# Token-major projections of a split-fp32 encoder layer: both weight parts in one 512-column matmul, halves added on VectorE, epsilon on GpSimd

## The chip, the cores and the metric

The kernel runs on one core of one Trainium2 chip. The metric is the time on the device in microseconds (us). Three runs of the kernel before took 1884.93, 1879.48 and 1882.31 us, so its median is 1882.31 us. The profile is of one more execution, whose span from the first to the last instruction is 1880.0 us.

Names of the engines: PE is TensorE's matmuls, PEld its weight loads, DVE is VectorE, ACT is ScalarE, POOL is GpSimd, SP is SyncE, which issues the DMAs.

## The reference

One encoder layer is applied to two groups (prompt and sample) of 1024 tokens and 1024 channels, with the same weights. Cut to what matters:

```
h = rms_norm(x, norm_g) * (1 + scale) + shift          # scale, shift, gate from w_ada
proj = einsum('bsd,de->bse', h, w_in)                  # one projection, split into
qa, ka, va, za, qb, kb, vb, zb, ga, gb = split(proj)   # 512,128,128,512, 512,512,512,512, 1024,1024
qa, ka = rope_2d(rms_norm(qa)), rope_2d(rms_norm(ka))  # per head of 64 channels, eps 1e-6
oa = gqa_attention(qa, ka, va) * silu(za)              # 8 query heads, 2 key heads
qb, kb = rope(rms_norm(qb)), rope(rms_norm(kb))        # 4 heads, two maps each
ob = rms_norm(diff_attention(qb, kb, vb, lam)) * silu(zb)
merged = sigmoid(ga) * (oa @ w_proj_a) + sigmoid(gb) * (ob @ w_proj_b)
y = x + gate * (merged @ w_out)
```

All data is float32. The kernel multiplies with a reduced float32 type and keeps the accuracy by splitting each operand into a high part and a low part (value minus high part): a product is high x high + high x low + low x high, three matmuls.

## The kernel before, in words

**The weave.** The two groups run one after the other. In each, a head computes K and V of branch A and half of branch A's queries, then the attention units run, woven with work that does not depend on them ("filler": the rest of the projections and the gate paths), then come the merge and the output projection. `weave` takes pieces of several generators in turn, by counts given in tables at the top; a generator's `yield` ends a piece. Afterwards a scheduler with its own model of the engines orders the instructions of each engine, and lets the attention's instructions go ahead by a priority. The order on each engine is fixed then; each engine works through its own in that order.

**Two kinds of projections.** The gate paths (`z_gen`, matmul at L764) hold a piece of the weights still and move 512 tokens; their result has channels on the partitions. The token-major projections (`proj_tt`, matmul at L574) hold 128 tokens still and move 256 weight columns; their result has tokens on the partitions, 128 tokens x 256 channels. A weight tile `w` has, for each of 8 chunks of 128 input channels, 256 columns of the high part and then 256 columns of the low part. For each chunk `proj_tt` issues three matmuls of 256 columns (L574): token high part x weight high part, token high part x weight low part, token low part x weight high part. All 24 of a tile add up in the same 256 columns of one PSUM bank. Each has its own weight load, also where two in a row hold the same tokens.

**How many.** Each group has 8 token tiles of K and V of branch A (`kva_gen`), 2 x 8 of branch A's queries (`qa_gen`), 4 x 8 of branch B's queries and keys (`qkb_gen`), 2 x 8 of branch B's values (`vb_gen`): 72, so 144 in the kernel, 3456 matmuls at L574. 112 of them (all but the values of B) go through `rms`.

**What follows a tile.** `rms`: ACT copies the bank into a row tile in SBUF (L591), ACT squares it (L592), DVE sums each head's squares (L595), DVE adds epsilon (L596), POOL raises to the power -0.5 (L597). `rope` (L620 to L626) and the products with the gains run on DVE in the head (`alone`) and on POOL later. Two tiles later `pairs_T` transposes the row on PE (L637) into a PSUM bank, from which ACT (L639) and DVE (L640) write the high and low parts of the queries and keys. `vb_gen` only copies (L749); in `kva_gen` V is a second copy out of the bank (L689).

**Banks.** Projections, transposes and some small products take turns in three PSUM banks (`ps_f`, tiles f); the scores have two double banks (`ps_s`, tiles s); the values of the attention one (`ps_a`). While `alone` holds, two in five of the gate-path and transposing tiles take an s bank. A bank that is still read cannot be written.

**The attention.** A score step is four 512-column matmuls (L798, L799), a maximum on DVE (L800, 1024 columns), a product (L801), the exponential on ACT (L802), and a transposition on DVE (L843) that goes through DMAs (L852) to the values' matmuls (L866, L883). There are 256 score steps.

Of the kernel before, what the change touches and what calls it, by code (L numbers as in the profile page):

```python
# [14 lines left out]
AF = mybir.ActivationFunctionType  # L15
ALU = mybir.AluOpType
# [9 lines left out]
HD = 64  # L26
EPS = 1e-6
# [62 lines left out]
def kernel(ctx: ExitStack, tc: tile.TileContext, t: dict):  # L90
    nc = tc.nc
# [17 lines left out]
    def nm(s):  # L109
        uid[0] += 1  # L110
        return f"{s}_{uid[0]}"
# [13 lines left out]
    def fbank():  # L125
        return ps_f.tile([P, 512], F32, tag="f", name=nm("f"))

    def utile():
        return upool.tile([P, 2048], F32R, tag="u", name=nm("u"))
# [24 lines left out]
    def rtile():  # L154
        return mtile("row", [P, 512], bufs=3)
# [18 lines left out]
    def behind(ins, other):  # L174
        dep = mybir.DependencyInfo(mybir.DependencyClass.NoSync, mybir.DependencyReason.DATA)
        tc.add_manual_dep(ins.ins, other.ins.name, dep)
# [30 lines left out]
    def load_w(pieces, early=False):  # L207

        w = wpool.tile([P, NCH, 2, 256], F32R, tag="w", name=nm("w"))
        sts = []  # L210
        for q in range(4):
            if early:
                if q % 2 == 0:
                    room = halves2(ptile())
                st = room[q % 2].rearrange("p (c n) -> p c n", c=2)
            else:
                st = spool.tile([P, 2, 256], F32, tag="st", name=nm("st"))
            sts.append(st)
            off = 0
            for src in pieces(q):  # L220
                n = src.shape[1]
                dma(st[:, :, off : off + n], src.rearrange("(c p) n -> p c n", p=P))
                off += n
            assert off == 256
            if not early:
                split_w(w, q, st)
        return (w, sts) if early else w

    def w_cols(mat, *cols):
        def pieces(q):  # L230
            return [mat[q * 256 : (q + 1) * 256, c : c + n] for c, n in cols]
        return pieces
# [330 lines left out]
    latest = [None]  # L563

    def proj_tt(ht, w, tt):
        ps = fbank()[:, :256]
        hh, hl = ht[tt // 4]
        sl = slice((tt % 4) * P, (tt % 4 + 1) * P)
        k = 0
        for c in range(NCH):  # L570
            if c in CUTS:
                yield 1
            for lt, wi in ((hh, 0), (hh, 1), (hl, 0)):
                ins = nc.tensor.matmul(ps, lt[c][:, sl], w[:, c, wi, :], start=(k == 0), stop=(k == 23))  # L574
                if latest[0] is None:
                    behind(ins, picked[0])
                latest[0] = ins
                k += 1
        return ps

    def by_turns(tt):

        return nc.vector if alone[0] else nc.gpsimd

    chained = [None, None]

    def rms(ps, nh, e, kept=None, first=0):
        n = nh * HD
        row = rtile()
        raw, sq = row[:, :n], row[:, 256 : 256 + n]  # L590
        nc.scalar.activation(raw, ps, AF.Copy)  # L591
        chained[0] = nc.scalar.activation(sq, raw, AF.Square, scale=1.0 / math.sqrt(HD))  # L592
        ss = tiny.tile([P, 4], F32, tag="ss", name=nm("ss"))[:, :nh]
        rs = kept if kept is not None else tiny.tile([P, 4], F32, tag="rs", name=nm("rs"))[:, :nh]
        nc.vector.tensor_reduce(out=ss, in_=sq.rearrange("p (h d) -> p h d", d=HD), axis=AX.X, op=ALU.add)  # L595
        nc.vector.tensor_scalar(out=ss, in0=ss, scalar1=EPS, scalar2=None, op0=ALU.add)  # L596
        nc.gpsimd.tensor_tensor(out=rs, in0=ss, in1=nhalf[:, :nh], op=ALU.pow)  # L597
        raw3 = raw.rearrange("p (h d) -> p h d", d=HD)
        if first < nh:
            e.tensor_tensor(  # L600
                out=raw3[:, first:], in0=raw3[:, first:],
                in1=rs[:, first:].unsqueeze(2).to_broadcast([P, nh - first, HD]), op=ALU.mult,
            )
        return raw3, sq.rearrange("p (h d) -> p h d", d=HD)

    def rope(x3, s3, cos, sin, half, e):

        nh = x3.shape[1]
        w = x3.shape[2]
        ng = w // (2 * half)  # L610
        c3 = mtile("rc", [P, 4, HD], bufs=1)[:, :nh, :w]
        if len(cos.shape) == 3:
            x4, s4, c4 = (t.rearrange("p (a m) d -> p a m d", a=2) for t in (x3, s3, c3))
            cs, sn = (t.unsqueeze(2).to_broadcast([P, 2, nh // 2, w]) for t in (cos, sin))
        else:
            x4, s4 = (t.rearrange("p h (g d) -> p h g d", g=ng) for t in (x3, s3))
            c4, cs = None, None
            sn = sin.rearrange("p (g d) -> p g d", g=ng).unsqueeze(1).to_broadcast([P, nh, ng, 2 * half])
        if c4 is None:
            e.tensor_tensor(out=c3, in0=x3, in1=cos.unsqueeze(1).to_broadcast([P, nh, w]), op=ALU.mult)  # L620
        else:
            e.tensor_tensor(out=c4, in0=x4, in1=cs, op=ALU.mult)
        for a in range(2):
            o, i = (slice(b * half, (b + 1) * half) for b in (a, 1 - a))
            e.tensor_tensor(out=s4[..., o], in0=x4[..., i], in1=sn[..., o], op=ALU.mult)
        chained[1] = e.tensor_tensor(out=x3, in0=c3, in1=s3, op=ALU.add)  # L626
# [3 lines left out]
    def pairs_T(x3, even, odd):  # L630


        nb = x3.shape[1] // 2
        ps = gbank()[:, : nb * P].rearrange("p (b n) -> p b n", b=nb)
        x = x3.rearrange("p (b two) d -> p b (two d)", two=2)
        for b in range(nb):
            nc.tensor.transpose(ps[:, b, :], x[:, b, :], ident)  # L637
        for dst, hi, lo in ((even, LO, HI), (odd, HI, LO)):
            nc.scalar.activation(dst[hi], ps[hi], AF.Copy)  # L639
            nc.vector.tensor_tensor(out=dst[lo], in0=ps[hi], in1=dst[hi].bitcast(F32), op=ALU.subtract)  # L640
# [3 lines left out]
    def pipelined(ht, w, front, back, fill=(TAIL_Z, TAIL_Z)):  # L644
        pend = []
        for tt in range(NTT):
            ps = yield from proj_tt(ht, w, tt)
            pend.append((tt, front(tt, ps)))
            if tt == NTT - 1 and not alone[0]:
                ends[:] = chained  # L650
            if len(pend) > LAG:
                back(*pend.pop(0))
            yield 1
        while pend:
            for _ in range(fill[alone[0]]):
                next(filler[0], None)
            yield 1
            back(*pend.pop(0))
        yield 1
# [14 lines left out]
    def v2(u):  # L674
        return u.rearrange("p (h n) -> p h n", h=2)

    def kva_gen(ht, out):
        w = kva_w.pop()[0] if kva_w else load_w(w_cols(w_in, (C_KA, 256)))
        k = v2(utile())
        u = utile().bitcast(F32)  # L680
        va = u[:, :1024].rearrange("p (n k d) -> p n k d", n=NTT, k=2)
        out["ka"], out["va"] = k, va
        out["rsA"] = u[:, 1024 : 1024 + 2 * NTT * 4].rearrange("p (a n h) -> p a n h", a=2, n=NTT)

        def front(tt, ps):
            e = by_turns(tt)
            x3, s3 = rms(ps[:, :128], 2, e)
            vp = ps[:, 128:256].rearrange("p (k d) -> p k d", k=2)
            nc.scalar.activation(va[:, tt], vp, AF.Copy)  # L689
            e.tensor_tensor(out=x3, in0=x3, in1=gka.unsqueeze(1).to_broadcast([P, 2, HD]), op=ALU.mult)  # L690
            rope(x3, s3, out["cosA"][:, tt], out["sinA"][:, tt], 16, e)
            return x3

        def back(tt, x3):
            sl = slice(tt * P, (tt + 1) * P)
            pairs_T(x3, k[:, 0:1, sl], k[:, 1:2, sl])

        yield from pipelined(ht, w, front, back, (0, 0))
# [44 lines left out]
    def vb_gen(ht, out, pr):  # L743
        w = load_w(w_cols(w_in, (C_VB + pr * 256, 256)))
        v = utile().bitcast(F32).rearrange("p (n h e) -> p n h e", n=NTT, h=2)
        out[2 * pr], out[2 * pr + 1] = v[:, :, 0], v[:, :, 1]
        for tt in range(NTT):
            ps = yield from proj_tt(ht, w, tt)
            nc.scalar.activation(v[:, tt].rearrange("p h e -> p (h e)"), ps, AF.Copy)  # L749
            yield 1  # L750


# [527 lines left out]
    for g in range(2):  # L1280
# [19 lines left out]

        phase(0, qa_gen(st, 1))
        phase(1, vb_gen(ht, st["vb"], 0), qkb_gen(st, 0))
        oT, mT = ([], []), ([], [])
        for h in range(4):
# [8 lines left out]
        first = chain(*[gated_gen(st, i, hf, oT[hf]) for i in range(2) for hf in range(2)])  # L1313
# [78 lines left out]
```

## Time and profile before

| | |
|---|---|
| three runs | 1879.48, 1882.31, 1884.93 us |
| the profiled execution, span | 1880.0 us |
| PE busy, DVE busy | 1836.5 us, 1222.3 us |
| ACT busy, POOL busy | 780.1 us, 607.1 us |
| matmuls in the trace, of them at L574 and at L764 | 10398, 3456, 2304 |
| granted TensorE clock, mean | 0.995 of full |

The profile lists groups of instructions with the names of the tiles they write and read, their number, their total busy time and the mean of one. The record of a matmul is longer than the step from one matmul to the next, because matmuls are pipelined: the step is read from rows that give a run of matmuls with its length. The profiled execution is told by its span; nothing before the first or after the last instruction is in it.

### The profile page before, as it was taken

The numbers are of one execution on the slowest core, as the hardware profiler recorded it, in microseconds if no ns is written. First come the engines' busy times: TensorE is split into PE (matmuls) and PEld (weight loads), VectorE is DVE, ScalarE is ACT, GpSimd is POOL, SyncE is SP. The second block draws the span as 40 slices with busy tenths as digits, with TensorE's granted clock in tenths as the row PEclk, the third lists the DMA queues.
The fourth block names the chain that finished last, engine by engine and source line by source line (L and its number), as shares of the span: only waits on it lengthen the run. The fifth ranks groups of instructions, "written<-read, shape, count | busy, mean of one in ns | idle before, by whom it ended". The sixth has DMA issues, their size and how long they took to land.

```text
span 1880.0 us, 29891 instructions
## 1 busy us (share of the span) xinstructions
PE 1836.5 (98%) x10398; PEld 1550.6 (82%) x10398; DVE 1222.3 (65%) x2016; ACT 780.1 (41%) x1544; POOL 607.1 (32%) x888
## 2 busy tenths in 40 slices
PE   6999999999999999999999999999999999999999
PEld 3798877888899977888889888888888898888887
DVE  5777766454777777347466687666357766663795
ACT  4544434344554444313223445344345545442241
POOL 1243311433454451221233333014354635222100
PEclk8999999999999999999999999999999999999999
DMA  9135776555444567754631567666524343675442
GB/s 324 57 94 160 208 198 178 146 168 163 111 127 113 162 188 219 244 152 140 206 131 52 156 177 204 189 186 188 158 68 141 106 129 103 176 247 173 128 127 92
DMA packets 283895, 295.46 MB, mean 157 GB/s; under 512 B 41952, under 2 KB 236640, under 8 KB 283744
## 3 DMA queue, kind: packets, MB, share of 16 engines
q1 hardware_dynamic: 283744, 293.54, 53.1%
q8 instruction: 83, 1.36, 0.3%
q14 instruction: 68, 0.56, 0.1%
HBM read 133.98 MB, written 42.01 MB: 94 GB/s over the span
## 4 chain that ended last, share of the span: by engine, by line
PE 68%; DMA 4%; issue 3%; DVE 3%; SPq 3%; POOL 2%; ACT 1%; ACTq 0%; DVEq 0%; POOLq 0%
PE f L764 15%; PE f L574 15%; PE f L1038 7%; PE a L883 5%; PE s L798 4%; PE s L799 4%; PE a L866 4%; PE s L1038 3%; PE f L1073 3%; PE s L1073 2%; PE f L1145 2%; SPq L852 1%; DMA q<-p 1%; DMA st<-in_w_in_dram 1%; PE s L1145 1%
## 5 line engine op out<-in xcount | busy, mean ns | idle before, releaser
L764 PE MATMUL f<-u,w 128*128 128x512 f32 x2232 | 565.1, 395 | 0.8 <-POOL w L197 0.4
L574 PE MATMUL f<-w,u 128*128 128x256 f32 x3456 | 478.6, 287 | 0.9 <-POOL w L197 0.4
L764 PEld LDWEIGHTS f<-u,w 128*128 128x128 f32 x2232 | 409.8, 188 | 82.6 <-POOL w L197 1.1
L574 PEld LDWEIGHTS f<-w,u 128*128 128x128 f32 x3456 | 452.3, 193 | 22.3 <-issue 3.5
L800 DVE TENSOR_REDUCE m<-s 128x1 f32<-128x1024 f32 x256 | 309.6, 1218 | 98.8 <-PE s L799 97.4
L197 POOL TENSOR_TENSOR w<-st,w 128x512 fp32r<-128x512 f32 x160 | 213.2, 1350 | 357.9 <-ACT w L195 342.1
L843 DVE STREAM_TRANSPOSE p<-p 128x1024 f32<-128x1024 f32 x192 | 237.7, 1243 | 87.9 <-ACT p L802 73.5
L802 ACT ACTIVATE p<-s,m,u 128x1024 f32<-128x1024 f32 x128 | 153.9, 1204 | 160.0 <-issue 57.8
L802 ACT ACTIVATE p<-s,m,rsB 128x1024 f32<-128x1024 f32 x128 | 154.0, 1204 | 118.7 <-DVE m L801 97.1
L799 PE MATMUL s<-u,sw 128*128 128x512 f32 x512 | 201.1, 397 | 0.0
L195 ACT ACTIVATE w<-st 128x512 fp32r<-128x512 f32 x184 | 108.2, 626 | 112.4 <-DMA st<-in_w_in_dram 97.5
L1038 PE MATMUL f<-u,w 128*128 128x512 f32 x552 | 131.0, 392 | 0.0
L883 PE MATMUL a<-q,u 128*128 128x256 f32 x512 | 126.5, 380 | 4.0 <-DMA q<-p 3.7
L597 POOL TENSOR_TENSOR rsB<-ss,nhalf 128x4 f32<-128x4 f32 x64 | 68.1, 1064 | 184.7 <-DVE ss L596 160.6
L866 PE MATMUL a<-q,u 128*64 128x256 f32 x1024 | 117.7, 382 | 3.6 <-DMA q<-p 2.9
L1038 PEld LDWEIGHTS f<-u,w 128*128 128x128 f32 x552 | 103.0, 188 | 21.1
L798 PE MATMUL s<-u 128*128 128x512 f32 x256 | 107.9, 425 | 2.7 <-ACT p L802 2.7
L799 PEld LDWEIGHTS s<-u,sw 128*128 128x128 f32 x512 | 96.5, 189 | 16.4
L640 DVE TENSOR_TENSOR u<-f,u 64x256 fp32r<-64x256 f32 (+1 forms) x198 | 81.3, 411 | 42.9 <-ACT u L639 37.5
L883 PEld LDWEIGHTS a<-q,u 128*128 128x128 f32 x512 | 93.5, 190 | 18.8 <-issue 3.4
L772 ACT ACTIVATE ev<-f 128x512 f32<-128x512 f32 x93 | 55.3, 595 | 128.5 <-PE f L764 72.5
L866 PEld LDWEIGHTS a<-q,u 128*64 128x64 f32 x1024 | 73.8, 137 | 40.3 <-issue 7.2
(221 smaller groups left out, 2174.6 us busy)
## 6 DMA issues: line engine op xcount, KB each, us to landing
q<-p SPq DMA_DIRECT2D x768, 128.0 KB, 2.6
st<-in_w_in_dram SPq DMA_DIRECT2D x132, 256.0 KB, 3.3
zd<-ev SPq DMA_DIRECT2D x96, 256.0 KB, 2.7
sw<-u SPq DMA_DIRECT2D x256, 64.0 KB, 2.0
u<-in_w_ada_dram SPq DMA_DIRECT2D x8, 1024.0 KB, 11.7
oo<-zd SPq DMA_DIRECT2D x64, 128.0 KB, 2.4
od<-oo SPq DMA_DIRECT2D x64, 128.0 KB, 2.4
st<-in_w_in_dram SPq DMA_DIRECT2D x64, 128.0 KB, 2.7
```

The lines of the kernel that those rows point to most:

```text
L195: hi = nc.scalar.activation(wh, st, AF.Copy)
L197: lo = e.tensor_tensor(out=wl, in0=st, in1=wh.bitcast(F32), op=ALU.subtract)
L574: ins = nc.tensor.matmul(ps, lt[c][:, sl], w[:, c, wi, :], start=(k == 0), stop=(k == 23))
L764: ins = nc.tensor.matmul(ps, w[:, c, wi, e * P : (e + 1) * P], rt[c], start=(k == 0), stop=(k == 23),)
L798: nc.tensor.matmul(s[:, sl], q, k[:, sl], start=True, stop=False)
L799: nc.tensor.matmul(s[:, sl], sw, k[:, sl], start=False, stop=True)
L800: nc.vector.tensor_reduce(out=m, in_=s, axis=AX.X, op=ALU.max, negate=True)
L802: nc.scalar.activation(pt.rearrange("p (j c a) -> p j c a", j=4, c=8), s.rearrange("p (c a j) -> p j c a", c=8, j=4), AF.Exp, bias=m, scal ...
L843: nc.vector.transpose(pt, pt)
L866: lambda k=k, m=m: nc.tensor.matmul(acc[(LO, HI)[m]], u["v"][:, k], pT[m][:, k], start=(k == 0), stop=(k == 7))
L883: nc.tensor.matmul(acc, u["v"][:, k], pT[:, k], start=(k == 0), stop=(k == 7))
L1038: nc.tensor.matmul(ps, w[:, c, wi, d * P : (d + 1) * P], o[:, oi, :], start=(k == 0), stop=(k == 11))
```

## The change

The token-major projections use a whole PSUM bank. The token high part meets both weight parts in one matmul of 512 columns (the two parts lie next to each other in `w`), which fills both halves of the bank; the token low part meets the weight high part in a matmul of 256 columns that adds into the second half. A chunk has two matmuls and two weight loads where it had three of each, a tile 16 where it had 24. The number of columns that go through PE is the same.

What follows must add the halves: ACT copies the first half to SBUF, and DVE adds the second half, out of PSUM, to it (`summed`). In `kva_gen` V is copied from the summed row, not from PSUM. The addition of epsilon moves from DVE to POOL.

```
     def proj_tt(ht, w, tt):
-        ps = fbank()[:, :256]
+        ps = fbank()
...
-            for lt, wi in ((hh, 0), (hh, 1), (hl, 0)):
-                ins = nc.tensor.matmul(ps, lt[c][:, sl], w[:, c, wi, :], start=(k == 0), stop=(k == 23))
+            both = w[:, c].rearrange("p s n -> p (s n)")
+            for lt, out, wt in ((hh, ps, both), (hl, ps[:, 256:], w[:, c, 0, :])):
+                ins = nc.tensor.matmul(out, lt[c][:, sl], wt, start=(k == 0), stop=(k == 15))
...
+    def summed(out, ps):
+
+        nc.scalar.activation(out, ps[:, :256], AF.Copy)
+        nc.vector.tensor_tensor(out=out, in0=out, in1=ps[:, 256:], op=ALU.add)
...
-    def rms(ps, nh, e, kept=None, first=0):
+    def rms(ps, nh, e, kept=None, first=0, vp=None):
...
-        nc.scalar.activation(raw, ps, AF.Copy)
+        summed(row[:, :256], ps)
+        if vp is not None:
+            nc.scalar.activation(vp, row[:, n:256].rearrange("p (h d) -> p h d", d=HD), AF.Copy)
...
-        nc.vector.tensor_scalar(out=ss, in0=ss, scalar1=EPS, scalar2=None, op0=ALU.add)
+        nc.gpsimd.tensor_scalar(out=ss, in0=ss, scalar1=EPS, scalar2=1.0, op0=ALU.add, op1=ALU.mult)
...
-            x3, s3 = rms(ps[:, :128], 2, e)
-            vp = ps[:, 128:256].rearrange("p (k d) -> p k d", k=2)
-            nc.scalar.activation(va[:, tt], vp, AF.Copy)
+            x3, s3 = rms(ps, 2, e, vp=va[:, tt])
...
-            nc.scalar.activation(v[:, tt].rearrange("p h e -> p (h e)"), ps, AF.Copy)
+            summed(v[:, tt].rearrange("p h e -> p (h e)"), ps)
```

In the changed kernel the lines from 574 on have other numbers: the matmul of `proj_tt` is L575, the copy L584, the addition of the halves L585, the sum of squares L603, epsilon L604, the power L605, the transposition L645, the score matmuls L804 and L805, the maximum L806.

The scheduler orders each engine anew. PE at one place of the first group, in the weave of branch B: f_6714 is a projection tile, f_6791 the next one, f_6768 a bank of transposes, s_6942 a score step. Before:

```order
L574 MATMUL f_6714<-w_6462,u_329 128x256
L637 MATMUL f_6768<-ident,row_6604 128x128 x2
L798 MATMUL s_6942<-u_5427 128x512
L799 MATMUL s_6942<-u_5427,sw_6709 128x512
L798 MATMUL s_6942<-u_5427 128x512
L799 MATMUL s_6942<-u_5427,sw_6709 128x512
L574 MATMUL f_6791<-w_6462,u_511 128x256 x2
```

The same two projection tiles of the changed kernel are f_6245 and f_6315; f_6292 is the bank of transposes, s_6452 and s_6480 are two score steps:

```order
L575 MATMUL f_6245<-w_6014,u_329 128x256
L804 MATMUL s_6452<-u_5091 128x512
L805 MATMUL s_6452<-u_5091,sw_6240 128x512
L804 MATMUL s_6452<-u_5091 128x512
L805 MATMUL s_6452<-u_5091,sw_6240 128x512
L804 MATMUL s_6480<-u_5092 128x512
L805 MATMUL s_6480<-u_5092,sw_6240 128x512
L804 MATMUL s_6480<-u_5092 128x512
L805 MATMUL s_6480<-u_5092,sw_6240 128x512
L645 MATMUL f_6292<-ident,row_6141 128x128 x2
L575 MATMUL f_6315<-w_6014,u_497 128x512
```

Between one projection tile and the next there stand eight score matmuls instead of four; the transposes have moved behind them.

DVE at the same place. Before, row_6754 is the SBUF row of the projection tile f_6714, m_6941 the maximum of the score step s_6942:

```order
L801 TENSOR_TENSOR m_6873<-m_6873,rsB 128x1
L640 TENSOR_TENSOR u_6484<-f_6687,u_6484 64x2x128
L800 TENSOR_REDUCE m_6941<-s_6942 128x1
L827 RECIPROCAL r_6882<-su_6872 128x1
L640 TENSOR_TENSOR u_6483<-f_6768,u_6483 64x2x128
L595 TENSOR_REDUCE ss_6757<-row_6754 128x4
L801 TENSOR_TENSOR m_6941<-m_6941,rsB 128x1
L596 TENSOR_SCALAR ss_6757<-ss_6757 128x4
```

In the changed kernel row_6277 is the row of f_6245, m_6451 the maximum of s_6452:

```order
L807 TENSOR_TENSOR m_6387<-m_6387,rsB 128x1
L585 TENSOR_TENSOR row_6277<-row_6277,f_6245 128x256
L806 TENSOR_REDUCE m_6451<-s_6452 128x1
L833 RECIPROCAL r_6396<-su_6386 128x1
L603 TENSOR_REDUCE ss_6281<-row_6277 128x4
L806 TENSOR_REDUCE m_6479<-s_6480 128x1
L807 TENSOR_TENSOR m_6451<-m_6451,rsB 128x1
```

The addition of the halves stands ahead of the maximum of the score step that PE does after the tile; the epsilon row is gone from DVE.

## The prediction

> **What bounds the kernel now.** I read the page's busy times first, then PE's waits, then the stretches, then the chain of work that ended last. The page gives the span and the share of each engine:
>
> ```profile
> span 1880.0 us, 29891 instructions
> PE 1836.5 (98%) x10398; PEld 1550.6 (82%) x10398; DVE 1222.3 (65%) x2016; ACT 780.1 (41%) x1544; POOL 607.1 (32%) x888
> ```
>
> PE has work at 98% of the time, the other engines at two thirds or less. Since matmul records overlap, that alone does not show that PE sets the end. The view of waits of PE does: these are the longest but for the ones of the start, and together they are 18.3 us of 1880.
>
> ```profile
> PE s L798 <- ACT p L802: 4.2, 6, 1.2
> PE a L883 <- DMA q<-p: 3.7, 4, 1.5
> PE f L637 <- POOL row L626: 3.4, 2, 3.2
> PE a L866 <- DMA q<-p: 2.9, 4, 1.3
> PE f L637 <- DVE row L626: 2.5, 2, 1.4
> PE s L637 <- DVE row L626: 1.6, 1, 1.6
> ```
>
> The other engines wait for PE instead. ACT's copy of a projection tile, in the view of all waits, stood ready 71 times and waited for the tile's last matmul:
>
> ```profile
> ACT row L591 <- PE f L574: 138.1, 71, 6.8
> ```
>
> By stretches (PE, PEld, DVE, ACT, POOL busy us, then granted clock, DMA share, GB/s) the head of the first group is the place where PE has most pauses and DVE least; the weave of branch B in the second group is typical of the rest:
>
> ```profile
> 46.00:120.00 74.00, 69.42 (x470) 63.05 (x470) 60.52 (x173) 36.74 (x102) 26.38 (x28) 0.98 0.17 51
> 1280.00:1600.00 320.00, 315.13 (x1921) 275.41 (x1921) 200.94 (x341) 152.84 (x309) 150.70 (x281) 1.00 0.45 125
> ```
>
> DVE is at 82% in the first and at 63% in the second, where PE is at 98% and the clock is full. So the kernel is a queue of matmuls, and what a matmul takes from PE counts nearly in full, as long as the work behind it keeps up.
>
> **What the matmuls lose.** How long a step from matmul to matmul is, I take from the chain of waits, which gives unbroken runs (start us, length us, count):
>
> ```profile
> 801.98 24.48 PE f L1038 x108
> ...
> 893.80 10.88 PE f L1073 x48
> ...
> 970.89 8.64 PE f L574 x72
> ...
> 1019.02 5.75 PE f L574 x48
> ```
>
> A 512-column matmul steps by 24.48 / 108 = 226.7 ns, and L1073 by the same 10.88 / 48; the 256-column one of the projections by 8.64 / 72 = 120.0 ns, and 5.75 / 48 = 119.8. Half of 226.7 is 113.3, so the narrow matmul costs 6.7 ns more than its half. Put otherwise, 256 columns more cost 106.7 ns, and 13.3 ns come with each matmul, wide or narrow. A chunk is now 3 x 120.0 = 360.0 ns. The changed chunk is one wide and one narrow, 226.7 + 120.0 = 346.7 ns: 13.3 ns less, the fixed part of the matmul that goes. With 144 tiles of 8 chunks, 1152 chunks, that is **15.3 us off PE**. That a narrow one next to a wide one keeps its 120 ns is seen where a projection tile is followed by a gate-path tile:
>
> ```profile
> 370.04 3.04 PE L574 MATMUL f<-w,u 128*128 128x256 f32 x24
> 372.91 0.40 PE L764 MATMUL f<-u,w 128*128 128x512 f32 x1
> ```
>
> 24 narrow steps, the last one to a wide matmul, take 2.87 us, 119.6 each. The two rows give ends for the saving: nothing, if the wide matmul took two narrow steps, and 360.0 - 1.5 x 226.7 = 20.0 ns a chunk, 23.0 us, if the narrow one took half a wide one. I take the sum of the two measured steps.
>
> The Trainium skill speaks against this size: "TensorE: Matmul & The Clock Gate", section "Back-to-back issue gap", gives a warm step of N / 2.4 + 2.5 ns. By it a chunk would go from 327.5 to 325.0 ns, and the change would save 2.9 us in all. The trace's steps of 226.7 and 120.0 ns do not agree with it: the part that does not grow with the columns is 13.3 ns here.
>
> The 1152 weight loads that go lie under matmuls and are worth nothing by themselves; nothing takes their place.
>
> **What is added.** The rows that are nearest to the new DVE addition (128x256, one operand in PSUM, one in SBUF), the removed epsilon, and the new POOL epsilon are these:
>
> ```profile
> L872 DVE TENSOR_TENSOR oo<-a,oo 128x256 f32<-128x256 f32 x32 | 13.3, 416 | 39.6 <-PE a L866 39.5
> L596 DVE TENSOR_SCALAR ss<-ss 128x4 f32<-128x4 f32 x96 | 21.3, 222 | 1.3
> L900 POOL TENSOR_SCALAR suB<-suB 128x8 f32<-128x8 f32 x8 | 2.5, 309 | 0.7
> L626 DVE TENSOR_TENSOR row<-rc,row x32: 280/424/1268, 56.0 to 1043.9; 128x128 f32<-128x128 f32 x16, 128x256 f32<-128x256 f32 x16
> ```
>
> L872 has the new addition's size and kinds of operands: 0.416 us. The far end is 1.27 us, the longest L626, of the same size with both operands in SBUF; I take 0.416, which is the same form. (The Trainium skill, "SBUF — State Buffer", section "Who interferes with whom", says that a DVE instruction with two SBUF inputs can be blocked by GpSimd and that one with a single SBUF input cannot; L626's 1268 beside its median of 424 agrees with the first half.) DVE gets 144 x 0.416 = 59.9 us more and loses at most 112 x 0.222 = 24.9, so 1222 becomes about 1257 us, 67% of the span. POOL gets 112 x 0.31 = 35 us, 34%. ACT keeps its count but for a wider first copy in the 16 tiles of K and V, at 41%. None of these totals reaches PE's; what can cost is the length of the chain behind a tile, at three places.
>
> *The bank.* A projection bank is now held until DVE has added: 0.42 us longer if DVE is free, and if DVE is in a transposition, up to this row's mean more:
>
> ```profile
> L843 DVE STREAM_TRANSPOSE p<-p 128x1024 f32<-128x1024 f32 x192 | 237.7, 1243 | 87.9 <-ACT p L802 73.5
> ```
>
> So 0.42 to 1.66 us. Where room was short before, PE's weight load was held by the copy alone, as here (the bank of f_6714, then f_6791):
>
> ```profile
> 648.29 0.38 ACT L591 ACTIVATE row<-f 128x256 f32<-128x256 f32 x1
> ...
> 648.73 0.42 PEld L574 LDWEIGHTS f<-w,u 128*128 128x128 f32 x3 [0.30 <-ACT row L591]
> ```
>
> The new order of PE puts eight score matmuls where four stood between these two tiles, four times 226.7 ns or 0.9 us more room, so the scheduler pays for most of the longer hold. The same addition stands ahead of the next score maximum on DVE: queued behind it are that maximum, ACT's exponential and the next use of the score bank. PE needs 0.9 us for the score step anyway, and the addition 0.42. I put 2 us on banks, and 0 to 8 as ends (nothing to 0.42 us at 19 tiles, one in eight).
>
> *The transposes.* Five waits of L637 for the row are in the waits of PE above, 7.5 us together. Their rows come later by the addition and by the epsilon, 0.42 + 0.31 - 0.22 = 0.5 us each: 2.5 us, with 0 to 5 as ends (they vanish by the new order, or there are ten).
>
> *The head.* DVE is nearly full where query tiles follow each other with nothing between. One period of PE, and DVE's work in it:
>
> ```profile
> 106.69 3.12 PE L574 MATMUL f<-w,u 128*128 128x256 f32 x24
> ...
> 107.17 0.42 DVE L620 TENSOR_TENSOR rc<-row,tab 128x256 f32<-128x256 f32 x1 [0.22 <-ACT row L591]
> ...
> 107.63 0.42 DVE L640 TENSOR_TENSOR u<-f,u 64x256 fp32r<-64x256 f32 x1
> 108.08 0.42 DVE L595 TENSOR_REDUCE ss<-row 128x4 f32<-128x256 f32 x1
> ...
> 108.53 0.17 DVE L596 TENSOR_SCALAR ss<-ss 128x4 f32<-128x4 f32 x1
> 108.61 0.51 DVE L625 TENSOR_TENSOR row<-row,tab 128x128 f32<-128x128 f32 x2
> 109.15 0.43 DVE L640 TENSOR_TENSOR u<-f,u 64x256 fp32r<-64x256 f32 x1
> 109.61 0.43 DVE L626 TENSOR_TENSOR row<-rc,row 128x256 f32<-128x256 f32 x1
> 109.78 3.11 PE L574 MATMUL f<-w,u 128*128 128x256 f32 x24
> ```
>
> The period is 109.78 - 106.69 = 3.09 us and DVE works 2.80 of it. With the change PE's period is 3.09 - 8 x 0.0133 = 2.98 and DVE's work 2.80 + 0.42 - 0.17 = 3.05: DVE is the slower by 0.07 us a tile. Only a few tiles follow each other like this, so DVE falls back by a few tenths of a microsecond and does not stop PE, whose transposes come two tiles later. In the stretch before, where PE pauses most, the addition lies on the way of the K tiles' rows. I put 1 us on the head of both groups, 0 to 4 as ends.
>
> **The sum.** -15.3 + 2 + 2.5 + 1 = -9.8 us, so the profiled execution's 1880.0 us would become 1870.2. The span lies 2.3 us under the median of the runs, so the prediction is **1872 us**. With the ends of the added costs alone it is 1867 to 1884.
>
> **The rivals.**
>
> *The chain takes more than PE saves (slower).* ACT copies, DVE adds, and only then is the bank free; DVE is in order and has 1.2 us instructions in it. If each of the 71 tiles whose copy waited for PE gave its 0.416 us on to PE, that is 29.5 us, and the time 1882.3 - 15.3 + 29.5 = 1896. It decides from 15.3 / 144 = 0.11 us of PE wait per tile. For it speaks that the head's DVE has no room; against it the small waits of PE for banks and rows now, and the new order.
>
> *The wide matmul takes two narrow steps.* Then 240 ns stand in place of 226.7, PE saves nothing, the added 5.5 us stay: 1888. Against it are the two runs at 226.7 ns, of the same kind of operands. The skill's rule above is the near end of this: 2.9 us saved, 1885.
>
> *The narrow matmul shrinks as well.* 113.3 ns beside a wide one: 23.0 us less, and with half of the added costs 1882.3 - 23.0 + 2.7 = 1862. Against it is the 119.6 ns row.
>
> *Only the heads gain.* In the weave the attention's own chain, scores, exponential, transposition, DMA, would set the pace, and PE's saving would turn into waits for it. The tiles outside the weave are 16 in each group, 32 of 144: 15.3 x 32 / 144 = 3.4 us, 1879. For it are the waits of PE for L802 and for q above; against it, they are under 11 us in all.
>
> **How the numbers follow.** Chances: my forecast 0.58, the longer chain 0.11, two narrow steps 0.07, the narrow one shrinks 0.12, only the heads 0.12. About 0.3%, 5.6 us, is what a measurement of this kernel tells from no change: under 1876.7 is faster, over 1887.9 slower. Of the forecast 0.54 is under 1876.7 and 0.04 above (added costs near their ends). Faster: 0.54 + 0.12 = 0.66. Same: 0.04 + 0.07 + 0.12 = 0.23. Slower: 0.11. The range goes from 1860, under the shrinking narrow matmul, to 1885, above the heads alone and the ends of the costs; it leaves out the longer chain and most of the two narrow steps.
>
> **What would show it.** In the changed profile, unbroken runs at L575 should step by 346.7 ns for two matmuls; PE's busy time should fall by about 15 us, DVE's rise by about 35 and POOL's by 35; the addition L585 should take 0.42 us. PE's waits for f banks and for rows at L645 should stay under 15 us together. I am wrong if the pair steps by 360 ns, if waits of PE for DVE's addition add up to more than the saving, or if the score matmuls at L804 begin to wait for ACT by tens of microseconds.

## The result, and the profile after

The forecast of 1872 us was wrong, in sign too. The changed kernel takes **1908.97 us** (median of four runs, 1906.6 to 1911.6) beside 1881.02 of four runs of the kernel before: a ratio of 1.0149 with the interval 1.0133 to 1.0166, or 28 us. The profiled execution has a span of 1909.8 us, 29.8 more than before.

The head of the page after:

```profile
span 1909.8 us, 27777 instructions
## 1 busy us (share of the span) xinstructions
PE 1841.7 (96%) x9246; PEld 1494.1 (78%) x9246; DVE 1257.0 (66%) x2048; ACT 785.3 (41%) x1544; POOL 630.3 (33%) x1000
```

DVE's 1257 us is the forecast's figure. PE's busy time did not fall by 15 us, it rose by 5, and its share fell from 98% to 96%: PE stands still more often, and what it does takes longer. The addition costs by itself what the rows of before said (0.413 us against the 0.416 of the forecast), POOL's epsilon less (0.223 us against 0.309):

```profile
L585 DVE TENSOR_TENSOR row<-row,f 128x256 f32<-128x256 f32 x112 | 46.1, 413 | 44.8 <-ACT row L584 43.0
...
L604 POOL TENSOR_SCALAR ss<-ss 128x4 f32<-128x4 f32 (+1 forms) x112 | 25.0, 223 | 285.5 <-DVE ss L603 242.0
```

The waits of PE after (engine, line, releaser: us in total, times, longest):

```profile
PE s L804 <- ACT p L808: 11.4, 10, 3.3
PE f L645 <- DVE row L634: 10.8, 4, 4.7
...
PE a L889 <- DMA q<-p: 5.2, 5, 2.0
...
PE f L575 <- DVE row L585: 2.7, 3, 1.8
PE f L575 <- DVE u L648: 2.6, 3, 1.1
```

The rival that I had on the slower side was a projection bank held by the addition: that is the fourth row, and it is 2.7 us. The two that grew are others: score matmuls that wait for ACT's exponential (4.2 before) and transposes in f banks that wait for a rope row of DVE (2.5 before). Both are few and long. The longest two of the second kind stand at the heads of the two groups. The timeline of the changed kernel at the first one (start us, length us):

```profile
87.05 0.27 PE L645 MATMUL s<-ident,row 128*128 128x128 f32 x1
...
87.72 0.42 DVE L585 TENSOR_TENSOR row<-row,f 128x256 f32<-128x256 f32 x1 [0.25 <-ACT row L584]
...
88.27 1.42 DVE L633 TENSOR_TENSOR row<-row,tab 128x64 f32<-128x64 f32 x2
88.29 2.54 POOL L197 TENSOR_TENSOR w<-st,w 128x512 fp32r<-128x512 f32 x2 [1.47 <-ACT w L195]
...
89.61 1.76 DVE L197 TENSOR_TENSOR w<-st,w 128x512 fp32r<-128x512 f32 x1
91.30 0.28 DVE L634 TENSOR_TENSOR row<-rc,row 128x128 f32<-128x128 f32 x1
...
91.72 0.30 PE L645 MATMUL f<-ident,row 128*128 128x128 f32 x1 [4.40 <-DVE row L634]
```

The addition takes 0.42 us of this. Most of the 4.40 us pause of PE is what stands on DVE between the addition and the rope's last step (L634): the rope's products (L633), which take 1.42 us beside POOL's work, and then a subtraction for a weight tile (L197), 1.76 us, which the scheduler has put ahead of the step that PE waits for. In the kernel before, the row goes straight through at this place:

```profile
81.77 0.35 DVE L625 TENSOR_TENSOR row<-row,tab 128x64 f32<-128x64 f32 x2
...
82.04 0.28 DVE L690 TENSOR_TENSOR row<-row,gka 128x128 f32<-128x128 f32 x1
82.24 0.28 DVE L626 TENSOR_TENSOR row<-rc,row 128x128 f32<-128x128 f32 x1
...
82.67 0.30 PE L637 MATMUL f<-ident,row 128*128 128x128 f32 x1 [1.05 <-DVE row L626]
```

The longest of the waits for the exponential is of the same make. On ACT two of a weight tile's copies (L195), each of which waits for its DMA, stand ahead of the exponential:

```profile
709.46 0.63 ACT L195 ACTIVATE w<-st 128x512 fp32r<-128x512 f32 x1 [1.33 <-DMA st<-in_w_in_dram]
...
710.86 0.63 ACT L195 ACTIVATE w<-st 128x512 fp32r<-128x512 f32 x1 [0.37 <-DMA st<-in_w_in_dram]
...
711.40 1.19 ACT L808 ACTIVATE p<-s,m,rsB 128x1024 f32<-128x1024 f32 x1
...
712.73 0.50 PE L804 MATMUL s<-u 128*128 128x512 f32 x1 [3.31 <-ACT p L808]
```

The product that this exponential needs (L807 on DVE) had been done since 708.1 us, so the exponential stood ready for 3.3 us behind the copies.

And a pause has an after-effect. The stretches of the changed kernel around these two kinds of pause (PE, PEld, DVE, ACT, POOL busy us, then the granted clock, DMA share, GB/s):

```profile
709.00:713.00 4.00, 0.69 (x5) 0.27 (x2) 1.59 (x4) 3.15 (x6) 3.02 (x3) 1.00 0.62 177
713.00:721.00 8.00, 8.00 (x27) 6.52 (x27) 4.11 (x7) 2.43 (x5) 0.34 (x1) 0.57 0.36 109
721.00:740.00 19.00, 19.00 (x88) 15.82 (x87) 13.02 (x19) 6.13 (x10) 2.54 (x4) 1.00 0.63 196
```

After 3.3 us without matmuls PE is granted 0.57 of its clock, as a mean over 8 us: 27 matmuls, at a busy time that reads as full. By the clock's records in the trace the changed kernel has 40.3 us at half clock from 40 us of the span on, before 10.9 us. In these stretches a 512-column step takes 426 ns where it takes 227 at full clock (run 8's 256-column step 213 where it takes 120), so a microsecond there loses a little under half a microsecond; counted as half, the 29.4 us are 14.7 us more. The other loss is PE's idle time. From 40 us on, the kernel before and then the changed one:

```profile
40.00:1880.00 1840.00, 1814.07 (x10289) 1539.47 (x10288) 1201.51 (x1979) 766.15 (x1520) 598.43 (x876) 1.00 0.53 153
```

```profile
40.00:1909.80 1869.80, 1819.34 (x9138) 1483.31 (x9136) 1236.22 (x2011) 771.35 (x1520) 621.67 (x988) 0.99 0.51 150
```

Idle is 1840.00 - 1814.07 = 25.9 us before and 50.5 after: 24.5 more, of which the two waits that grew are 15.5. The wide matmul's saving, measured on a run of 19 pairs of the changed kernel, is smaller than forecast but there:

```profile
641.60 6.85 PE L575 MATMUL f<-w,u 128*128 128x256 f32 x38
648.29 1.02 PE L889 MATMUL a<-q,u 128*128 128x256 f32 x4
```

6.69 us for 19 pairs is 352 ns a pair where three narrow ones took 360: 8 ns by 1152 chunks, 9 us. The account closes: 24.5 of idle and 14.7 of clock, less 9 of matmuls, is 30 us for the 29.8 of the spans. The same account misses by about 3 us in runs 7 and 8 below, so closing this well is in part luck. What remains to be told is whether these pauses come from the new instructions or only from the new order.

### The profile page after: what moved, and what is told of

Read it like the earlier page. It is cut to its first block, busy times and chain, and to the rows that moved or that the text cites. A ratio compares the mean times of both kernels' runs of the same rounds, so it can differ in the third digit from the quotient of the medians.

```text
span 1909.8 us, 27777 instructions
## 1 busy us (share of the span) xinstructions
PE 1841.7 (96%) x9246; PEld 1494.1 (78%) x9246; DVE 1257.0 (66%) x2048; ACT 785.3 (41%) x1544; POOL 630.3 (33%) x1000
## 5 line engine op out<-in xcount | busy, mean ns | idle before, releaser
L575 PE MATMUL f<-w,u 128*128 128x512 f32 (+1 forms) x2304 | 457.9, 345 | 7.3 <-DVE row L585 2.7
L575 PEld LDWEIGHTS f<-w,u 128*128 128x128 f32 x2304 | 370.0, 191 | 67.2 <-DVE row L585 4.0
L806 DVE TENSOR_REDUCE m<-s 128x1 f32<-128x1024 f32 x256 | 308.7, 1217 | 78.9 <-PE s L805 76.3
L197 POOL TENSOR_TENSOR w<-st,w 128x512 fp32r<-128x512 f32 x160 | 215.9, 1368 | 393.3 <-ACT w L195 373.0
L805 PE MATMUL s<-u,sw 128*128 128x512 f32 x512 | 203.0, 399 | 0.0
L195 ACT ACTIVATE w<-st 128x512 fp32r<-128x512 f32 x184 | 108.1, 625 | 113.1 <-DMA st<-in_w_in_dram 99.7
L604 POOL TENSOR_SCALAR ss<-ss 128x4 f32<-128x4 f32 (+1 forms) x112 | 25.0, 223 | 285.5 <-DVE ss L603 242.0
L804 PE MATMUL s<-u 128*128 128x512 f32 x256 | 108.9, 429 | 9.3 <-ACT p L808 9.2
L889 PEld LDWEIGHTS a<-q,u 128*128 128x128 f32 x512 | 96.1, 192 | 24.5 <-issue 6.8
L805 PEld LDWEIGHTS s<-u,sw 128*128 128x128 f32 x512 | 97.2, 190 | 18.8 <-issue 1.5
L648 DVE TENSOR_TENSOR u<-f,u 64x256 fp32r<-64x256 f32 (+1 forms) x198 | 81.3, 411 | 44.7 <-ACT u L647 39.7
L804 PE MATMUL s<-u,u 128*128 128x512 f32 x256 | 103.5, 407 | 2.2 <-ACT p L808 2.2
```

The source lines that it names most:

```text
L195: hi = nc.scalar.activation(wh, st, AF.Copy)
L197: lo = e.tensor_tensor(out=wl, in0=st, in1=wh.bitcast(F32), op=ALU.subtract)
L575: ins = nc.tensor.matmul(out, lt[c][:, sl], wt, start=(k == 0), stop=(k == 15))
L804: nc.tensor.matmul(s[:, sl], q, k[:, sl], start=True, stop=False)
L805: nc.tensor.matmul(s[:, sl], sw, k[:, sl], start=False, stop=True)
L806: nc.vector.tensor_reduce(out=m, in_=s, axis=AX.X, op=ALU.max, negate=True)
```

## The experiments

Theory A, the rival of the prediction: the addition makes the chain from bank to row longer, and PE waits. Theory B: any changed cost makes the scheduler lay out another order for all engines, while the weave's counts and pacing numbers stay what they were for before's; the other order loses by itself. Ratios are to the kernel before on the same chip, with 95% intervals.

**1. Epsilon back on DVE.** The changed kernel, one line undone.

```
-        nc.gpsimd.tensor_scalar(out=ss, in0=ss, scalar1=EPS, scalar2=1.0, op0=ALU.add, op1=ALU.mult)
+        nc.vector.tensor_scalar(out=ss, in0=ss, scalar1=EPS, scalar2=None, op0=ALU.add)
```

> The changed kernel with epsilon back on VectorE; wide matmuls and the addition stay. Theory A (the chain: the addition between the copy and the square holds banks and rows back, PE waits for that): epsilon is a side matter, about 1905 us, within 5 us of the changed kernel's 1909. Theory B (the order: any changed cost lets the scheduler lay out all engines anew, and the tables were fitted to the order of before, so a new order loses by waits that have little to do with the addition): somewhere from 1890 to 1915, with pauses of PE at other places than in the changed kernel.

Measured 1913.31 us, 1.0159 [1.0142, 1.0176]. The move of epsilon is not what made the changed kernel slow. Both theories' ranges hold this time, so the run does not decide between them.

**2. Epsilon alone.** The kernel before with the same line changed, nothing else.

```
-        nc.vector.tensor_scalar(out=ss, in0=ss, scalar1=EPS, scalar2=None, op0=ALU.add)
+        nc.gpsimd.tensor_scalar(out=ss, in0=ss, scalar1=EPS, scalar2=1.0, op0=ALU.add, op1=ALU.mult)
```

> The kernel before with epsilon moved to GpSimd and nothing else. Theory A: PE's work and the banks are as before, one 0.22 us instruction goes from one chain link to the next, so 1881 to 1885 us. Theory B: the scheduler's new order costs here as well, 1888 to 1905 us.

Measured 1906.56 us, 1.0122 [1.0107, 1.0137]. There is no addition and no wide matmul here, and 23 us are lost, 22 over the end of A's range and 2 over the end of B's: A can't be the whole cause. But run 1, without this edit, loses as much, so the edit isn't a cost that adds to others either. This is what B says.

**3. The addition without the wide matmul.** 24 narrow matmuls a tile; the two low products go to the second half of the bank, and DVE adds. Epsilon on DVE.

```
-            for lt, wi in ((hh, 0), (hh, 1), (hl, 0)):
-                ins = nc.tensor.matmul(ps, lt[c][:, sl], w[:, c, wi, :], start=(k == 0), stop=(k == 23))
+            for lt, out, wt in ((hh, ps[:, :256], w[:, c, 0, :]), (hh, ps[:, 256:], w[:, c, 1, :]), (hl, ps[:, 256:], w[:, c, 0, :])):
+                ins = nc.tensor.matmul(out, lt[c][:, sl], wt, start=(k == 0), stop=(k == 23))
```

> The addition without PE's saving: 24 matmuls of 256 columns as before, but the two products with a low part go to the bank's second half, and VectorE adds the halves; epsilon on VectorE. Theory A: before plus all that the chain costs, 1909 + 15 = about 1924 us. Theory B: no sum holds, 1890 to 1920 us; the places of the pauses differ from those of the changed kernel.

Measured 1927.32 us, 1.0225 [1.0203, 1.0247]. This is 3 us from A's figure and 7 us over the end of B's range: by itself the run speaks for A.

**4. The wide matmul without the addition.** The changed kernel with epsilon on DVE and without L585; the second half of the bank is left out of the result.

```
     def summed(out, ps):
         nc.scalar.activation(out, ps[:, :256], AF.Copy)
-        nc.vector.tensor_tensor(out=out, in0=out, in1=ps[:, 256:], op=ALU.add)
```

> PE's saving without the addition: wide matmuls, but the bank's second half is left out of the result (the products with the low parts are dropped); epsilon on VectorE. Theory A: before minus 15 us, 1866 us, since no chain is longer. Theory B: minus 15 us and a new order's loss, 1872 to 1895 us.

Measured 1893.55 us, 1.0058 [1.0037, 1.0079]. From run 1 to run 4 the addition is worth 1.0159 - 1.0058, or 19 us; from 3 to 1 the wide matmul saves 0.0066, or 12 us. Even so, run 4 has PE's saving and no addition, and is slower than before. Each of these kernels has an order of its own, so the parts must be compared in one order.

**5. All of the change in before's order.** The order of all five engines is written out: a table of instruction numbers for each, and a chain of dependencies without semaphores from each number to the next. Each addition is put on DVE where the trace of before has the end of the copy that it follows; POOL's epsilon stands ahead of its power.

```
+    for text in ORDER.values():
+        names = np.frombuffer(zlib.decompress(base64.b85decode(text)), np.uint16).tolist()
+        dep = mybir.DependencyInfo(mybir.DependencyClass.NoSync, mybir.DependencyReason.DATA)
+        for x, y in zip(names, names[1:]):
+            tc.add_manual_dep(nc.find_inst_by_name(f"I-{y}"), f"I-{x}", dep)
```

> The changed kernel, every instruction of it, but each engine's order is held to that of the kernel before: a wide matmul stands where the first of its three stood, VectorE's addition where ACT's copy ended in the trace of before, epsilon ahead of the power. Theory A (the addition's longer chain costs about 20 us whatever the order): 1883 - 15 + 20 = about 1888 us. Theory B (the scheduler's new order costs some 25 us): 1868 to 1880 us, the nearer to 1868 the less the chain costs.

Measured 1891.84 us, 1.0046 [1.0027, 1.0066]: 19 us of the 28 are gone, and no instruction of the change has been taken out. But it is 12 us over the end of B's range, and A's figure of 1888 is the nearer one: in before's order, too, the change costs 9 us where it was to save. So the order is most of the loss, as B says, and the added work costs something without it, as A says. PE's waits in this kernel (its transposes are L656, its score matmuls L815):

```profile
PE f L656 <- DVE row L645: 3.9, 1, 3.9
...
PE s L815 <- ACT p L819: 3.1, 3, 2.6
...
PE f L586 <- DVE row L596: 2.4, 2, 1.7
```

The two that grew in the changed kernel, 11.4 and 10.8 us, are 3.1 and 3.9 here; the wait for the addition (L596) is 2.4 as it was 2.7.

**6. Epsilon alone in before's order.** Run 2's kernel with that table.

```
+    for text in ORDER.values():
...
```

> The kernel before with epsilon on GpSimd alone, as in the run that took 1906 us, but in the order of the kernel before. Theory A (epsilon on GpSimd is what cost there, by GpSimd's longer chain): about 1905 us again. Theory B: 1881 to 1886 us.

Measured 1881.08 us, 0.9993 [0.9979, 1.0007]. The 23 us of run 2 are gone. Epsilon on POOL and the holding of an order by such a table cost nothing together; they were not run apart.

**7. The wide matmul without the addition in before's order.** Run 4's kernel with that table; the second half of the bank is left out of the result.

```
+    for text in ORDER.values():
...
```

> Wide matmuls without the addition (the products with the low parts are left out of the result), epsilon on VectorE, in the order of the kernel before. Theory A and B both say that only the order stands between the 1893 us of the same kernel in its own order and the full saving of PE: 1866 to 1870 us. If it stays at 1880 or more, the wide matmuls cost something of their own.

Measured 1878.83 us, 0.9981 [0.9970, 0.9992]. This is the one kernel of the study that is faster than before: by 4 us, of the 9 that the steps give. Both theories had 1866 to 1870, and it is 9 us over that.

**8. Before's instructions in the changed kernel's order.** The kernel before, no instruction changed, with a table that follows the order of the changed kernel (the narrow pair where a wide matmul stands; epsilon on DVE right behind the sum of squares).

```
+    for text in ORDER.values():
...
```

> The other way round: the kernel before, its 256-column matmuls and no addition, with each engine held to the order that the scheduler gave the changed kernel. Theory A (the order is harmless, the addition costs): 1880 to 1887 us. Theory B: the order alone costs, 1900 to 1915 us, although no instruction differs from the kernel before.

Measured 1914.28 us, 1.0166 [1.0147, 1.0185]. This is the study's main run: the order alone costs 31 us, without an addition, without a wide matmul, without POOL's epsilon. PE's waits (score matmuls L809, transposes L648):

```profile
PE s L809 <- ACT p L813: 14.3, 11, 3.7
PE f L648 <- DVE row L637: 10.7, 3, 4.5
```

They are the changed kernel's two. The head of the first group shows the same pause, with nothing added:

```profile
88.78 0.35 DVE L636 TENSOR_TENSOR row<-row,tab 128x64 f32<-128x64 f32 x2
89.31 2.94 POOL L208 TENSOR_TENSOR w<-st,w 128x512 fp32r<-128x512 f32 x2 [1.66 <-ACT w L206]
89.78 1.35 DVE L208 TENSOR_TENSOR w<-st,w 128x512 fp32r<-128x512 f32 x1 [0.65 <-ACT w L206]
...
91.05 1.34 DVE L637 TENSOR_TENSOR row<-rc,row 128x128 f32<-128x128 f32 x1
...
92.54 0.30 PE L648 MATMUL f<-ident,row 128*128 128x128 f32 x1 [4.03 <-DVE row L637]
```

The weight tile's subtraction (L208 here) stands ahead of the rope's last step again. Idle from 40 us on is 46.5 us in this kernel, 20.6 over before:

```profile
40.00:1914.00 1874.00, 1827.48 (x10288) 1547.02 (x10287) 1204.10 (x1979) 764.69 (x1520) 597.54 (x876) 0.99 0.52 150
```

It has 44.4 us at half clock there, 33.5 more than before, worth 16.8: together 37 us for a span that is 34.0 longer, so the account is 3 us too large here.

**9. Another order for before.** One pacing number of the weave.

```
-BEHIND = 1.4
+BEHIND = 1.45
```

> The kernel before with one pacing number of the weave, BEHIND, at 1.45 in place of 1.4. No instruction differs from before in kind, size or count; the scheduler lays them in another order. Theory B (before's order is fitted, any re-laid order loses by itself): 1890 to 1910 us. Theory A (only the addition costs; other orders are as good): 1879 to 1885 us.

Measured 1894.78 us, 1.0059 [1.0039, 1.0079]. A small move of a number that stands for no work costs 11 us. Idle from 40 us on is 33.5 us, 7.5 over before:

```profile
40.00:1893.50 1853.50, 1820.03 (x10288) 1544.93 (x10286) 1201.67 (x1979) 764.34 (x1520) 599.06 (x876) 0.99 0.52 152
```

**10. The addition off the chain.** Run 5's kernel, with the sum written to a scrap tile: the bank is held as long and DVE works as much, but all that follows reads the bare copy (the second half is left out of the result). The scrap tile is bfloat16; the addition into it takes 0.421 us in the median, as run 5's takes 0.420.

```
-        nc.vector.tensor_tensor(out=out, in0=out, in1=ps[:, 256:], op=ALU.add)
+        nc.vector.tensor_tensor(out=scrap, in0=out, in1=ps[:, 256:], op=ALU.add)
```

> The changed kernel in before's order of every engine, with the addition written to a scrap tile: the square, the rope and V read the bare copy, so the second half of the bank is left out of the result. The bank is held as long and DVE works as much as with the addition; only the link copy, addition, next step is gone. If the 13 us of the addition in before's order (1891.8 against 1878.8) are the link in the chain, this gives 1879 to 1882 us; if they are the longer hold of the bank or DVE's fuller queue, 1889 to 1892 us. Theory B says nothing on this, since the order is before's.

Measured 1887.06 us, 1.0027 [1.0016, 1.0038], between the two forecasts. Run 7, which differs by leaving the addition (and POOL's epsilon) out, is at 0.9981: so the hold of the bank and DVE's time cost 0.0046, or 9 us. The link costs the rest to run 5, 0.0019 or 4 us, and the intervals of these two overlap: that part is not settled.

**11. The heads narrow.** Run 5's kernel, but the 32 tiles outside the weave (`alone`) keep 24 narrow matmuls and no addition.

```
+            if alone[0]:
+                for lt, wi in ((hh, 0), (hh, 1), (hl, 0)):
+                    ins = nc.tensor.matmul(ps[:, :256], lt[c][:, sl], w[:, c, wi, :], start=(k == 0), stop=(k == 23))
...
+        if not alone[0]:
+            nc.vector.tensor_tensor(out=out, in0=out, in1=ps[:, 256:], op=ALU.add)
```

> The changed kernel in before's order of every engine, but the 32 projection tiles that stand outside the weave keep 24 narrow matmuls and no addition; the other 112 have the wide matmul and the addition. If the addition's cost lies in the heads, where DVE had 0.3 us of room in a period of 3.09 (4.8 us were lost there by the first score step of group 0): 1884 to 1887 us. If it is spread over the weave: 1890 to 1893 us.

Measured 1886.90 us, 1.0021 [1.0009, 1.0034]. The heads carry 0.0025 or 5 us of the addition's cost, with an interval that overlaps run 5's, though they are 32 tiles of 144; with the 2 us that these tiles give up of the matmul's saving (9 x 32 / 144), 7. The profiled executions agree: around the two heads (40 to 130 and 960 to 1060 us) PE is idle for 12.5 us in run 5, 7.6 in run 11 and 6.5 before.

**12. Another order for the changed kernel.** Run 9's edit in the changed kernel.

```
-BEHIND = 1.4
+BEHIND = 1.45
```

> The changed kernel with the pacing number BEHIND at 1.45 in place of 1.4, the number that cost the kernel before 11 us (1894.8 against 1882.5): no instruction differs from the changed kernel, and the scheduler lays a third order. If 1909 is what the changed instructions cost in any order that is not held to before's, this is 1906 to 1912 us. If 1909 is one order's luck (theory B), it leaves that range by more than 4 us in either direction, and stays over the 1891.8 us of the changed instructions in before's order: 1893 to 1904, or over 1913.

Measured 1907.11 us, 1.0115 [1.0086, 1.0144]. This speaks against B as far as B says luck: a third order loses 22 us, about as much, and the same two waits lead:

```profile
PE f L645 <- DVE row L634: 12.3, 4, 4.7
PE s L804 <- ACT p L808: 9.3, 7, 2.5
```

## Why the prediction was wrong

**The step that failed** is the treatment of the order. The prediction read at one place that eight score matmuls stand where four stood, and took it for a gain: "so the scheduler pays for most of the longer hold". From there on it costed the changed instructions in before's order, as if their neighbours stayed. Run 8 shows the price of what was left out: 31 us for the order with no instruction changed. By the changed kernel's own path it is 1.0149 - 1.0046 (run 5), 19 us. The two differ, so the costs of order and addition don't simply add; both show that the largest term of the sum was missing. In the pauses that are shown above, an instruction that waits for a DMA or for another engine (a weight tile's copy or subtraction) now stands ahead of the step that PE waits for. The order is known before anything runs, but whether these places could have been priced from it was not tried.

In one order the sum can be followed by steps: wide matmul -0.0019 (run 7), addition and epsilon +0.0065 (run 7 to run 5), new order +0.0103 (run 5 to the changed kernel): -4 + 12 + 19 us, to the 28 measured.

**The matmul, -15.3 us.** Right in kind, too large. The prediction added a step of 226.7 ns and one of 120.0. The pair takes 352 in the run of 38, so 8 ns are saved a chunk, not 13.3: 9 us. In the trace after, a narrow step behind a wide one is 117 ns, a wide step ahead of a narrow one 233 (medians): the steps from the unbroken runs of one size did not carry over to the mixture. The chunk of before, by the median of its steps, is 120.0 x 3 as stated. Of the 9 us, run 7 shows 4 in the time. Its idle time from 40 us on is 26.9 us, 0.9 over before, and it has 2.8 us more at half clock, worth 1.4; some 3 us of the difference stay unexplained. Its row for that stretch:

```profile
40.00:1875.90 1835.90, 1809.03 (x9138) 1480.37 (x9137) 1203.10 (x1980) 768.62 (x1520) 597.81 (x876) 1.00 0.52 153
```

**The added costs, 2 + 2.5 + 1 = 5.5 us with 17 as the far end.** In before's order they are 12 us, within the ends and twice the middle. The head was sized at 1 us, with 0 to 4: run 11 has 5 to 7 for the two heads. The prediction saw DVE the slower there, by 0.07 us in a period, and took it for harmless because the transposes come two tiles later; which pause of the head comes from that is not shown. That the banks cost 2 can't be checked alone; run 10 gives 9 us for hold and DVE's time together, heads included. In run 5's trace the pauses that name the addition are 2.4 us; so most of its cost must show under the names of other rows.

**Epsilon.** Right in before's order: the time is the same within 0.0014 (run 6). In an order that is laid anew it is 23 us (run 2), though 112 instructions of 0.2 us moved to an engine with two thirds of its time free.

**The rivals.** "The chain takes more than PE saves", at 1896 with 0.11, had the sign, and in before's order it is what happens: run 5 is slower than before by 9 us. It doesn't explain the 28. "Two narrow steps" and "the narrow matmul shrinks as well" are both refuted by 352 ns. No rival named the order.

**What stays open.** Why before's order is so good is not shown. That the weave's tables were fitted to it would explain why all eight kernels with other orders (1, 2, 3, 4, 8, 9, 12 and the changed one) are slower than before, and why the three of them (2, 4 and the changed one) that were also run in before's order are faster there; the runs show only that they are. Run 12 has a loss of the same size by the same two waits, so with the addition the scheduler seems to fall into these again; whether its model's prices do that was not tried. Nor was it tried to place the additions by hand where DVE has room.

## What to carry to other kernels

Where a scheduler lays out the instructions, the price of an edit has two parts: what the instructions cost, and what the new order costs. Hold the old order for the changed instructions, and the new order for the old ones, before any term is called the cause. In a kernel whose bound engine is 98% busy, look in the new order for instructions with a long wait (on a DMA, on a slower engine) that have moved ahead of something which the bound engine waits for; here fourteen pauses of two kinds, with half clock behind the longer ones, outweighed the 0.5% that the steps saved.

## What the runs showed of the hardware

**Half clock behind short pauses.** In the changed kernel a pause of 2.03 us of PE (it ends at 589.68) is followed by 0.57 of the clock:

```profile
587.00:590.00 3.00, 0.97 (x6) 0.62 (x5) 2.94 (x4) 0.57 (x2) 2.87 (x7) 1.00 0.79 230
590.00:594.00 4.00, 4.00 (x13) 3.22 (x12) 1.56 (x4) 2.79 (x6) 2.54 (x3) 0.57 0.65 175
```

In the kernel before, one of 3.2 us in the first row is followed by the full clock:

```profile
1390.00:1394.00 4.00, 0.79 (x5) 0.32 (x4) 3.90 (x6) 0.73 (x2) 4.00 (x7) 1.00 0.44 116
1394.00:1402.00 8.00, 8.00 (x49) 7.21 (x50) 6.31 (x13) 4.58 (x10) 5.71 (x14) 1.00 0.42 107
```

So the length of a pause alone doesn't decide. In the clock's records of these two kernels the stretches at half clock are 3.41 or 6.83 us long (one at the start 13.65), and they start on a grid of 3.41 us. The pause of 2.03 us lies inside one step of that grid (587.06 to 590.47), in which PE has matmuls for 0.40 of the time; the pause of 3.2 us is split between two steps, with 0.52 and 0.54. Counted over all 14 traces from 70 us on, for steps at full clock: under 0.44, all 38 steps are followed by half clock; from 0.44 to 0.54, 12 of 34; above, 2 of 7319. So where a pause lies against the grid goes with what it costs; no run moved a pause to test it. The Trainium skill, "TensorE: Matmul & The Clock Gate", section "What's actually happening", has a free-running window of 3413 ns, and these lengths agree with it. Its section "HAM oscillation — how this bites in real kernels" asks for no idle gap over about 3.4 us; by the pause of 2.03 us that is too mild here.

**VectorE and GpSimd on the same work.** In the changed kernel DVE's subtraction for a weight tile takes 0.69 us in the median, and 1.76 us where POOL does the same beside it (the pause at 87 us); smallest, median and longest in ns:

```profile
L197 DVE TENSOR_TENSOR w<-st,w x24: 673/692/1776, 50.5 to 1814.9; 128x512 fp32r<-128x512 f32 x24
```

In run 8's rows the rope's last step, 0.28 us elsewhere, takes 1.34 beside POOL's. This agrees with what the Trainium skill, "SBUF — State Buffer", section "Who interferes with whom", says of DVE instructions with two SBUF inputs, which the prediction cited. Here it stands on PE's path: it is part of the head's pause in both kernels.
